# Attention weights rounded and split by two transfers instead of by engine instructions

## The chip, the cores and the metric

The kernel runs on one core of a Trainium2 chip. The metric is the device time of one execution in microseconds (us). The median of the runs decides. Next to it stands one profiled execution, whose trace gives the start and the duration of every instruction.

The engines of a core each work through their own instructions in order: PE (matmul), PEld (PE's loading of weights, beside the matmuls), DVE (vector), ACT (scalar and activation functions), POOL (general purpose) and SP (issues transfers). They wait for each other by semaphores. POOL and ACT can issue transfers as well.

## The reference

Two layers over a sequence of 512 tokens with 1024 channels. Per layer:

```
h = RMSNorm(x)
q, k, v, gates of 16 heads = h @ w_in           # one combined projection
A (8 heads): compressed, selected and window attention, gated
B (4 heads): stick-breaking attention           C (4 heads): forgetting attention
x = x + concat(A, B, C) @ w_out
x = x + cross_attention(RMSNorm(x), RMSNorm(mem), w_mq, w_mk, w_mv, w_mo)
x = x + (silu(gate) * val) @ w_down,  gate, val = conv3(RMSNorm(x) @ w_up)
```

and a last RMSNorm. All is in fp32.

## The kernel before

PE multiplies in a rounded fp32 format (`fp32r`). To keep the precision, each operand is split into a rounded part and the rest that rounding leaves, and each product is three matmuls: weight-high by input-high, weight-high by input-low, weight-low by input-high. A "weight" below is a block of a weight matrix, 128 partitions by 384 to 1120 columns, and takes two buffers of the kind `w`: `h` (rounded) and `l` (rest). There are NW = 8 of them (line 26). `load_w` (line 494) makes a weight in pieces of at most 560 columns: SP fetches a piece into a `raw` buffer (`wr` in the trace; six of them), ACT or DVE copies it to `h` with rounding, DVE or POOL writes raw minus `h` to `l`. Weights of 1024 to 1120 columns come in two pieces, those of 384 and 512 columns in one.

Per layer the weights are: 16 tiles of `w_in` (`job_t`) and three wider blocks, two weights each (`job_n`); the output projection in three parts, `wa` with eight weights of 512 columns and `wb` with eight of 384 (`job_wo`, line 1448), and one more of 1024; eight of the cross-attention, of 1024; then the feed-forward weights through `Prefetch` (line 519), two ahead.

Nothing is issued as written. Every operation is first recorded in a list (`Plan.add`, with a cost for its engine). `Plan.run` (line 207) then sets the order: for each engine it takes the ready operation of the lowest number in the list, and if none of the low ones is ready, a later one. An operation that needs a new buffer gets it if one of its kind is free and `room` finds that the operations ahead of it in the list can still go on with what remains. At the end it creates the buffers and issues the operations in that order (line 349). A buffer's name is its own number, an underscore, and a number that counts the buffers in the order of their creation. So `w1056_927` was created 927th, although the list names it late.

`run_items` mixes the projections (as filler) with the attention items, so that PE has matmuls of a projection while DVE and ACT work on a softmax.

Of the kernel before, what the change touches and what calls it, by code (L numbers as in the profile page):

```python
# [12 lines left out]
FR = mybir.dt.float32r  # L13
BF = mybir.dt.bfloat16
AF = mybir.ActivationFunctionType
OP = mybir.AluOpType
# [6 lines left out]
NF = 22  # L23
NH = 11

NSLOT, NW, NRAW = 67, 8, 6
WRAW = 560
EPS = 1e-6
NEG = -1e30
# [4 lines left out]
FPART, FNUM = 4, 2  # L34
# [318 lines left out]
class Engine:  # L353
# [17 lines left out]
    def __getattr__(self, name):  # L371
        def call(out, *args, **kw):
            full = lambda v: v.full if isinstance(v, Buf) else v
            out = full(out)
            args = [full(a) for a in args]
            kw = {k: full(v) for k, v in kw.items()}
            outs, ins = [out], [a for a in args if isinstance(a, View)]
            for k, v in kw.items():
                if isinstance(v, View):
                    (outs if k == "accum_out" else ins).append(v)  # L380
            real = lambda v: v.ap() if isinstance(v, View) else v
            eng = self.plan.engines[self.key]

            def fn():
                return getattr(eng, name)(real(out), *[real(a) for a in args], **{k: real(v) for k, v in kw.items()})  # L385

            if name == "activation" and args[1] in TABLED:
                ins = ins + [self.plan.table.full]
            if name == "dma_start":
                src = args[0]  # L390
                outs = [v for v in outs if isinstance(v, View)]
                size = ins[0] if ins else out
                nbytes = size.size() * (size.p1 - size.p0) * 4
                near = outs and ins and not any(v.buf.dram for v in outs + ins)
                cost = 1000 if self.key == "POOL" else 650 if near else 475
                if self.only:
                    return name, outs, ins, fn, cost, nbytes / 355.0
                return self.plan.add(self.key, name, outs, ins, fn, cost, nbytes / 355.0)
            if name == "matmul":
                n = args[1].size()  # L400
                c = max(64, n) / 2.4
                if args[1].buf.dtype == FT or (args[1].buf.dtype == FR and n < 256):
                    c *= 4
                if not kw.get("start"):
                    ins = ins + [out]
                return self.plan.add("PE", name, outs, ins, fn, max(c, 104) + 3)
            if name == "transpose":
                return self.plan.add("PE", name, outs, ins, fn, 110)
            cost = self._cost(name, out, ins, kw)
            if self.only:  # L410
                return name, outs, ins, fn, cost, 0
            return self.plan.add(self.key, name, outs, ins, fn, cost)
        return call
# [38 lines left out]
def tile_hybrid_trunk(ctx: ExitStack, tc: tile.TileContext, xT, memT, win_t, win_n0, win_n1, win_n2,  # L452
# [6 lines left out]
    plan = Plan(tc, {"slot": (NSLOT, sb), "w": (NW, sb), "raw": (NRAW, sb), "kcx": (1, sb),  # L459
                           "s32": (24, sb), "s128": (8, sb), "ps": (8, ps)})  # L460
    ve, se, te, gp, sy = [Engine(plan, k) for k in ("DVE", "ACT", "PE", "POOL", "SP")]
# [3 lines left out]
    def nm(s):  # L465
        uid[0] += 1
        return f"{s}{uid[0]}"
# [19 lines left out]
    def f(ap):  # L487
        return ap.bitcast(FT)
# [2 lines left out]
        te.matmul(o, a, b, start=start, stop=stop, skip_group_check=on)  # L491


    def load_w(src, n, shape, parts=None):

        h, l = [plan.buf("w", (128, n), FR, nm("w")).full for _ in range(2)]
        a, b = shape
        c = parts or -(-n // WRAW)
        if a == 1:
            cuts = [(src[:, :, k * b // c:(k + 1) * b // c], k * b // c, (k + 1) * b // c) for k in range(c)]  # L500
        else:
            cuts = [(src[:, k * a // c:(k + 1) * a // c], k * a // c * b, (k + 1) * a // c * b) for k in range(c)]

        def piece(v, c0, c1):
            def fn():
                raw = plan.buf("raw", (128, c1 - c0), FT, nm("wr"))
                sy.dma_start(raw, v)
                split(h[:, c0:c1], l[:, c0:c1], raw)
            return fn

        w = h.rearrange("p (a b) -> p a b", a=a), l.rearrange("p (a b) -> p a b", a=a)
        todo = [piece(*k) for k in cuts]
        if parts:
            return w, todo
        for t in todo:
            t()
        return w

    class Prefetch:
# [3 lines left out]

        def get(self, i):
            while self.n < min(len(self.specs), i + 1 + self.ahead):
                self.got[self.n] = load_w(*self.specs[self.n])
                self.n += 1
            return self.got.pop(i)

# [1065 lines left out]
    nrm = Norm(gn[:, 0, 0])  # L1595
    first, pieces = {}, []
    for tl in FIRST:
        first[0, tl], p = load_w(win_t[0, tl], 1024, (8, 128), FPART)
        pieces += p
    sy.dma_start(gn, gains)  # L1600
    for j in range(8):
# [105 lines left out]
```

## Time and profile before

| | us |
|---|---|
| median of three runs | 1523.96 |
| lowest run | 1519.58 |
| profiled execution, device time | 1528.35 |
| its span, first to last instruction | 1526.6 |
| PE busy | 1434.0 |
| DVE busy | 1142.1 |
| ACT busy | 678.0 |
| POOL busy | 428.7 |

The span runs through: start (0 to 58 us), attention of layer 1 mixed with its projections (to 309), the rest of the output projection (to 323), cross-attention (to 402), feed-forward (to 768), then the same for layer 2 (780 to 1512), and the output. An engine that is busy for less than the whole span is not the bound in general, but can be in a stretch. A matmul's row shows 0.39 us, but the next one starts 0.23 us after it, since matmuls are pipelined.

### The profile page before, as it was taken

How to read it: one execution, taken by the hardware profiler on the slowest of the kernel's cores; microseconds unless marked ns; L12 is line 12 of the kernel's file. 1: busy time of each engine (PE TensorE's matmuls, PEld its weight loads, DVE VectorE, ACT ScalarE, POOL GpSimd, SP SyncE). 2: the span in 40 equal slices, each digit the busy share in tenths (PEclk: the TensorE clock that was granted, in tenths of full speed). 3: DMA queues.
4: the chain of work that ended last, by engine and by line, in shares of the span. 5: the costliest groups of instructions: out<-in, count | busy, mean ns of one | idle time of the engine just before them, and what ended most of it. 6: DMA issues, size and time to landing. Idle time of an engine off the chain costs nothing.

```text
span 1526.6 us, 21518 instructions
## 1 busy us (share of the span) xinstructions
PE 1434.0 (94%) x7414; PEld 1171.9 (77%) x7414; DVE 1142.1 (75%) x2198; ACT 678.0 (44%) x1498; POOL 428.7 (28%) x357
## 2 busy tenths in 40 slices
PE   7789899888899999999999989999889999999997
PEld 5768687677788788888888767876878887888886
DVE  7997856888988835887577777576988786378864
ACT  5547566646632212323333656774584322132321
POOL 4440312342422212221143312133533221122211
PEclk9899999999999999999999999999999999999999
DMA  8630223134122233332443112312312223323232
GB/s 254 201 100 29 70 77 101 31 104 132 56 97 95 69 103 107 97 100 79 147 125 103 34 45 79 114 49 72 113 44 85 90 84 93 108 89 95 80 95 75
DMA packets 88205, 142.05 MB, mean 93 GB/s; under 512 B 12208, under 2 KB 35040, under 8 KB 88096
## 3 DMA queue, kind: packets, MB, share of 16 engines
q1 hardware_dynamic: 85280, 137.67, 29.1%
q0 software_dynamic: 1184, 1.44, 0.4%
q10 hardware_dynamic: 1632, 1.57, 0.3%
q8 instruction: 58, 0.95, 0.3%
q14 instruction: 51, 0.42, 0.1%
HBM read 125.04 MB, written 8.39 MB: 87 GB/s over the span
## 4 chain that ended last, share of the span: by engine, by line
PE 67%; DVE 23%; issue 4%; ACT 3%; DMA 1%; SPq 0%; POOL 0%; DVEq 0%; ACTq 0%; POOLq 0%
PE pj L385 37%; PE S L385 23%; PE acc L385 4%; DVE w L385 4%; DVE cv L385 3%; PE T L385 3%; DVE hl L385 2%; ACT cv L385 1%; DVE x L385 1%; DVE u L385 1%; DVE P L385 1%; DVE sp L385 1%; DMA wr<-in_dram 1%; DVE cs L385 1%; DVE sa L385 1%
## 5 line engine op out<-in xcount | busy, mean ns | idle before, releaser
L385 POOL TENSOR_TENSOR w<-wr,w 128x512 fp32r<-128x512 f32 (+4 forms) x217 | 304.6, 1409 | 825.4 <-PE pj L385 339.3
L385 PE MATMUL pj<-hh,w 128*128 128x512 f32 (+1 forms) x1376 | 433.0, 385 | 13.1 <-ACT hh L385 7.7
L385 PEld LDWEIGHTS pj<-hh,w 128*128 128x128 f32 x1376 | 255.5, 191 | 65.2 <-ACT hh L385 8.6
L385 ACT ACTIVATE w<-wr 128x512 fp32r<-128x512 f32 (+3 forms) x296 | 165.4, 585 | 277.4 <-PE pj L385 176.8
L385 PE MATMUL pj<-hl,w 128*128 128x512 f32 (+1 forms) x688 | 263.2, 383 | 3.1 <-DVE hl L385 2.9
L385 DVE TENSOR_TENSOR w<-wr,w 128x512 fp32r<-128x512 f32 (+3 forms) x251 | 195.0, 791 | 94.4 <-PE S L385 44.9
L385 PE MATMUL S<-hh,w 128*128 128x512 f32 (+1 forms) x736 | 230.7, 385 | 0.0
L385 DVE SCALAR_TENSOR_TENSOR cv<-u,conv,cv 128x510 f32<-128x510 f32 (+1 forms) x176 | 155.7, 887 | 69.8 <-ACT cv L385 66.6
L385 PEld LDWEIGHTS S<-hh,w 128*128 128x128 f32 x736 | 137.2, 189 | 29.6
L385 PEld LDWEIGHTS pj<-hl,w 128*128 128x128 f32 x688 | 131.3, 191 | 30.8 <-DVE hl L385 6.5
L385 DVE CAST w<-wr 128x512 fp32r<-128x512 f32 (+3 forms) x172 | 75.3, 453 | 97.0 <-issue 43.3
L385 ACT ACTIVATE cv<-u,conv 128x512 f32<-128x512 f32 x88 | 71.5, 815 | 171.1 <-DVE u L385 171.1
L385 PE MATMUL S<-hl,w 128*128 128x512 f32 (+1 forms) x368 | 141.4, 384 | 0.0
L385 PE MATMUL pj<-oh,w 128*128 128x512 f32 (+1 forms) x320 | 103.3, 374 | 18.1 <-DVE x L385 13.5
L385 PE MATMUL S<-gh,w 128*128 128x512 f32 (+1 forms) x396 | 114.3, 368 | 0.0
L385 PE MATMUL pj<-gh,w 128*128 128x512 f32 x352 | 113.4, 395 | 0.3 <-DVE gh L385 0.3
L385 ACT ACTIVATE P<-P,nmx 128x128 f32<-128x128 f32 (+3 forms) x160 | 88.5, 555 | 39.6 <-DVE nmx L385 39.3
L385 DVE CUSTOM_DVE_ANT_0 P<-S,maskq 128x128 f32<-128x128 f32 (+3 forms) x160 | 71.8, 483 | 40.1 <-PE S L385 37.8
L385 PEld LDWEIGHTS pj<-oh,w 128*128 128x128 f32 x320 | 60.3, 191 | 32.9 <-DVE x L385 15.8
L385 PEld LDWEIGHTS S<-gh,w 128*128 128x128 f32 x396 | 71.4, 188 | 13.4
L385 PEld LDWEIGHTS S<-hl,w 128*128 128x128 f32 x368 | 69.5, 189 | 15.0
L385 PE MATMUL pj<-w,hh 128*128 128x280 f32 (+2 forms) x384 | 79.4, 301 | 0.2 <-POOL w L385 0.2
(273 smaller groups left out, 2558.5 us busy)
## 6 DMA issues: line engine op xcount, KB each, us to landing
wr<-in_dram SPq DMA_DIRECT2D x292, 256.0 KB
wr<-in_dram SPq DMA_DIRECT2D x112, 192.0 KB
wr<-in_dram SPq DMA_DIRECT2D x48, 128.0 KB
x<-in_dram SPq DMA_DIRECT2D x16, 256.0 KB
dh<-dh SPq DMA_DIRECT2D x20, 128.0 KB
wr<-in_dram SPq DMA_DIRECT2D x8, 280.0 KB
wr<-in_dram SPq DMA_DIRECT2D x8, 260.0 KB
cw<-in_dram SPq DMA_DIRECT2D x8, 256.0 KB
```

The lines of the kernel that those rows point to most:

```text
L385: return getattr(eng, name)(real(out), *[real(a) for a in args], **{k: real(v) for k, v in kw.items()})
```

## The change

`load_w` is given a new body. POOL issues a transfer that brings the whole weight from memory into `h` and rounds it on the way; ACT copies `h` with the sign changed into `l`, in two halves; POOL issues a second transfer of the same weight, which adds it onto `l`. So `l` is again the weight minus its rounded part. No `raw` buffer, cast or subtract is used. The old body is kept as `split_w`, for the feed-forward weights (through `Prefetch`) and for the four tiles that are fetched at the very start. There are ten `w` buffers instead of eight and 62 buffers of the common kind (`slot`) instead of 67; the planner's cost for an issue by POOL goes from 1000 to 560 ns.

```
-NSLOT, NW, NRAW = 67, 8, 6
+NSLOT, NW, NRAW = 62, 10, 6
...
-                cost = 1000 if self.key == "POOL" else 650 if near else 475
+                cost = 560 if self.key == "POOL" else 650 if near else 475
...
-    def load_w(src, n, shape, parts=None):
+    def load_w(src, n, shape):
+        h, l = [plan.buf("w", (128, n), FR, nm("w")).full for _ in range(2)]
+        w = [v.rearrange("p (a b) -> p a b", a=shape[0]) for v in (h, l)]
+        gp.dma_start(w[0], src)
+        for c in range(2):
+            s_ = slice(c * n // 2, (c + 1) * n // 2)
+            se.activation(l[:, s_], f(h[:, s_]), AF.Copy, scale=-1.0)
+        gp.dma_start(w[1], src, accum_op=OP.add)
+        return w
+
+    def split_w(src, n, shape, parts=None):
...
-                self.got[self.n] = load_w(*self.specs[self.n])
+                self.got[self.n] = split_w(*self.specs[self.n])
...
-        first[0, tl], p = load_w(win_t[0, tl], 1024, (8, 128), FPART)
+        first[0, tl], p = split_w(win_t[0, tl], 1024, (8, 128), FPART)
```

The planner makes a new order out of it. Three places:

POOL in layer 1 at the end of the output projection, before (`w838`, `w842`, `w849`: the `l` buffers of `wb` weights):

```order
L385 TENSOR_TENSOR sp789_3289<-sp787_3241,sp788_3281 128x384
L385 TENSOR_TENSOR w838_3302<-wr839_2969,w837_3002 128x384
L385 TENSOR_TENSOR sb805_3335<-sp802_3271 128x256
L385 TENSOR_TENSOR sp811_3349<-sp809_3304,sp810_3342 128x384
L385 TENSOR_TENSOR sp809_3304<-sp809_3304,sb805_3335 128x256
L385 TENSOR_TENSOR w842_3373<-wr843_3015,w841_3225 128x384
L385 TENSOR_TENSOR w849_3487<-wr850_3090,w848_3368 128x384
```

and POOL at the same place now (`w802`, `w805`, `w808`, `w811` are `h` buffers of `wb` weights, `w797`, `w803`, `w806` `l` buffers, which the transfer adds onto):

```order
L385 DMA w802_3396<-in_7_dram 128x384
L385 DMA w794_3393<-in_7_dram 128x384
L385 DMA w805_3422<-in_7_dram 128x384
L385 DMA w797_3420<-in_7_dram 128x384
L385 DMA w808_3439<-in_7_dram 128x384
L385 DMA w803_3437<-in_7_dram 128x384
L385 DMA w811_3456<-in_7_dram 128x384
L385 DMA w806_3454<-in_7_dram 128x384
```

Subtracts among other work have become pairs of issues, the rounding transfer of one weight before the adding one of the weight ahead of it. By the creation numbers `w803` and `w808` come together, after `w797` and `w805`.

PE at that place before (`wb` weights `w837`/`w838` and `w841`/`w842`):

```order
L385 MATMUL pj840_3440<-oh819_3346,w837_3002 128x512
L385 MATMUL pj840_3440<-ol820_3377,w837_3002 128x512
L385 MATMUL pj840_3440<-oh819_3346,w838_3302 128x512
L385 MATMUL pj844_3455<-oh697_2929,w841_3225 128x512
L385 MATMUL pj844_3455<-ol698_2934,w841_3225 128x512
L385 MATMUL pj844_3455<-oh697_2929,w842_3373 128x512
```

and PE there now (`w796`/`w797` is one weight, `w802`/`w803` the next, `w808` the `h` of the weight next but one):

```order
L385 MATMUL pj798_3379<-oh722_3093,w797_3420 128x512
L385 MATMUL pj798_3379<-oh777_3305,w796_3351 128x512
L385 MATMUL pj798_3379<-ol778_3319,w796_3351 128x512
L385 MATMUL pj798_3379<-oh777_3305,w797_3420 128x512
L385 MATMUL pj810_3444<-oh661_2873,w808_3439 128x512
L385 MATMUL pj810_3444<-ol662_2881,w808_3439 128x512
L385 MATMUL pj804_3408<-oh661_2873,w803_3437 128x512
L385 MATMUL pj804_3408<-oh722_3093,w802_3396 128x512
```

`w803` gets its buffer when `w796` is read for the last time. Between that matmul and the first that reads `w803` stand three.

POOL early in layer 1, now, among the projections (`w186`, `w207` are `l` buffers of attention weights; `w1056` belongs to the first feed-forward weight):

```order
L385 DMA dl168_900<-dl168_900 64x512
L385 DMA dl170_907<-dl170_907 64x512
L385 TENSOR_TENSOR w1056_927<-wr1058_394,w1055_780 128x512
L385 DMA w186_923<-in_2_dram 128x1024
L385 DMA rot15_77<-u180_939 8x512 x2
```

and the first subtract of a feed-forward weight on POOL before, which stands behind the subtracts of the cross-attention's weights:

```order
L385 TENSOR_TENSOR w990_3986<-wr992_3637,w989_3890 128x512
L385 TENSOR_TENSOR w1069_4015<-wr1071_3895,w1068_3915 128x512
L385 TENSOR_TENSOR w1073_4020<-wr1074_3928,w1072_3980 128x512
L385 TENSOR_TENSOR sta955_3961<-qm953_3952,sta955_3961 64x256
L385 TENSOR_TENSOR w1126_4141<-wr1127_3999,w1125_4111 128x512
```

So the first feed-forward weight was created 4111th and 4141st, and is created 780th and 927th now.

## Rows read from the trace of the kernel before

**Rows 1.** The page, busy us, share of the span and instructions.

```profile
PE 1434.0 (94%) x7414; PEld 1171.9 (77%) x7414; DVE 1142.1 (75%) x2198; ACT 678.0 (44%) x1498; POOL 428.7 (28%) x357
```

**Rows 2.** Busy time by stretch: start:end, length, engines, granted clock, DMA share, GB/s.

```profile
core 0: us, PE busy (x) PEld busy (x) DVE busy (x) ACT busy (x) POOL busy (x), PEclk, DMA share, GB/s
58.00:116.00 58.00, 51.28 (x272) 41.86 (x272) 52.04 (x121) 29.06 (x76) 24.41 (x23) 0.94 0.51 156
116.00:309.00 193.00, 182.14 (x1086) 142.76 (x1085) 137.92 (x364) 127.72 (x320) 44.09 (x35) 1.00 0.21 62
309.00:323.00 14.00, 14.00 (x61) 11.16 (x62) 10.20 (x13) 3.62 (x6) 5.93 (x5) 1.00 0.43 138
323.00:402.00 79.00, 63.83 (x461) 58.92 (x460) 73.75 (x144) 51.88 (x138) 35.36 (x35) 0.92 0.32 102
402.00:768.00 366.00, 365.04 (x1639) 298.28 (x1638) 264.07 (x406) 112.60 (x185) 81.52 (x59) 1.00 0.32 98
780.00:1055.00 275.00, 257.81 (x1486) 206.20 (x1485) 199.37 (x494) 156.83 (x391) 77.36 (x64) 0.98 0.23 69
1069.00:1158.00 89.00, 74.24 (x539) 69.09 (x538) 83.81 (x170) 56.48 (x149) 39.10 (x38) 0.92 0.25 76
1158.00:1512.00 354.00, 353.60 (x1542) 286.48 (x1541) 247.44 (x376) 99.80 (x159) 76.85 (x54) 1.00 0.28 88
```

**Rows 3.** Waits of PE: for whom, us in total, times, longest.

```profile
PE pj L385 <- DVE x L385: 18.4, 12, 3.1
PE T L385 <- DVE P L385: 9.4, 10, 1.4
...
PE pj L385 <- DVE w L385: 1.1, 2, 0.6
...
PE pj L385 <- POOL w L385: 0.2, 1, 0.2
```

**Rows 4.** Groups of instructions: count, busy us, mean ns; idle before.

```profile
L385 POOL TENSOR_TENSOR w<-wr,w 128x512 fp32r<-128x512 f32 (+4 forms) x217 | 304.6, 1409 | 825.4 <-PE pj L385 339.3
L385 DVE TENSOR_TENSOR w<-wr,w 128x512 fp32r<-128x512 f32 (+3 forms) x251 | 195.0, 791 | 94.4 <-PE S L385 44.9
L385 DVE CAST w<-wr 128x512 fp32r<-128x512 f32 (+3 forms) x172 | 75.3, 453 | 97.0 <-issue 43.3
...
L385 ACT ACTIVATE w<-wr 128x512 fp32r<-128x512 f32 x190 | 114.0, 625 | 148.2 <-PE pj L385 102.7 <-issue 24.5 <-PE S L385 7.8
...
L385 ACT ACTIVATE w<-wr 128x256 fp32r<-128x256 f32 x21 | 8.7, 413 | 22.2 <-PE pj L385 17.5 <-issue 3.5 <-DMA wr<-in_dram 1.2
```

**Rows 5.** Tiles `rot`, then `dl`: POOL's issues, ns min/median/max, and landing.

```profile
L385 POOL DMA_DIRECT2D rot<-u x22: 497/514/546, 33.0 to 847.1; - x22
...
DMA to landing us min/median/max: 1.8/2.4/5.3
...
L385 POOL DMA_DIRECT2D dl<-dl x4: 527/537/558, 98.8 to 990.4; - x4
...
DMA to landing us min/median/max: 2.3/3.8/4.0
```

**Rows 6.** The page, transfer queue of SP: packets, MB, share of 16 engines.

```profile
q1 hardware_dynamic: 85280, 137.67, 29.1%
```

**Rows 7.** Timeline at the end of `wb`: start, duration, instruction [idle before].

```profile
320.44 0.39 PE L385 MATMUL pj<-ol,w 128*128 128x512 f32 x1
...
320.67 0.63 PE L385 MATMUL pj<-oh,w 128*128 128x512 f32 x2
...
320.92 0.64 ACT L385 ACTIVATE w<-wr 128x512 fp32r<-128x512 f32 x1 [1.43 <-PE pj L385]
...
321.63 1.29 POOL L385 TENSOR_TENSOR w<-wr,w 128x512 fp32r<-128x512 f32 x1 [0.75 <-ACT w L385]
...
321.94 1.25 DVE L385 CAST w<-wr 128x512 fp32r<-128x512 f32 x1
```

**Rows 8.** The chain that ended last, matmuls of 256 columns: start, us, count.

```profile
349.40 5.49 PE pj L385 x48
```

## What the change is expected to do to the time

> **What bounds the kernel now.** I read the page's busy shares first: PE is busy 1434.0 of 1526.6 us, DVE 75%, ACT 44%, POOL 28% [rows 1]. Then the table by stretches [rows 2]: in the feed-forward stretches (402 to 768 and 1158 to 1512) PE is free for about 1 us. In the attention stretches (116 to 309, and 780 to 1055 in layer 2) it is free for 11 us of 193 and 17 of 275. The 14 us from 309 to 323, which are the second part of the output projection (`wb`, eight weights), have no gap at all. Only in the cross-attention stretches (323 to 402, 1069 to 1158) is DVE the fuller engine, 73.75 of 79.00 us, with PE free for 15. Last the waits [rows 3]: PE waits for `x` and `P`; for a weight it waits 1.1 us (DVE) and 0.2 us (POOL) in the whole run. So the weights come in time today, and the work that makes them lies beside PE's wherever DVE is not the bound.
>
> **What is removed.** Of 468 pieces, 148 go (attention weights; SP's `wr` transfers fall from 468 to 320). By the order on each engine DVE loses 74 casts and 76 subtracts, ACT 74 copies, POOL 72 subtracts. By mean durations that is DVE 74 x 0.453 + 76 x 0.791 = 94 us and POOL 72 x 1.409 = 101 us [rows 4]. Where it could pay is PE's free time in the stretches with such weights: 6.7 + 10.9 + 15.2 us in layer 1 and 17.2 + 14.8 in layer 2, together 64.8 [rows 2]. Bounds of the gain: 0 (PE hardly waits for weights) and 65. I take 50, near the upper end, because whatever of this free time a lighter DVE leaves over can serve the new waits below; it can't be lost twice.
>
> **What is added.** 90 weights, each with two transfers issued by POOL and two ACT copies. POOL's issue: the rows of `rot` and `dl` show about 0.5 us each [rows 5], 180 x 0.54 = 97 us, as much as it loses, and beside PE. ACT: 116 halves of 512 columns (some a little wider) at 0.625, 32 of 256 at 0.413, 32 of 192 at some 0.36 (estimate, on the line through the other two) [rows 4], 97 us more, less the 74 copies that go: ACT, busy for 128 of 193 us at most [rows 2], has room. The weights' bytes are read twice: about 38 MB more beside 142, where the DMA engines are busy for 0.21 to 0.51 of the time [rows 2]. None of this is the price. The price is time from slot to weight, and how many weights are under way.
>
> **How many are under way.** A weight needs two of the `w` slots, 8 before and 10 now. But the attention weights no longer pass through the six `raw` buffers, so SP fetches feed-forward pieces as soon as layer 1 begins, and engines with nothing of lower number to do split them. The POOL rows in the section on the change show `w1056`, a feed-forward weight, made as tile 927, while PE reads it after the whole cross-attention. Six slots go so in layer 1 (`w1055`, `w1056`, `w1059`, `w1060`, `w1063`, `w1064`, all made by tile 1667) and six in layer 2 (`w2542` to `w2554`). Four slots stay: two weights under way, where before it was four. The negated copy of the next weight can't be written before PE has finished with the one ahead of it: it takes that one's slot.
>
> **Time from slot to weight.** Before: the raw piece lies ready, ACT copies in 0.625 us and POOL subtracts in 1.409, or DVE does both in 0.453 + 0.791 [rows 4]: 1.2 to 2.1 us. Now: handovers, two ACT halves, issue and landing of the adding transfer. The handovers I take as 0.35 us: 0.16 because a matmul ends 0.39 us after its start while the next follows after 0.23, and 0.07 for each step, as from ACT's end at 321.56 to POOL's start at 321.63 [rows 7]. The landing no row shows. Nearest are POOL's own transfers: 16 KB land 1.8 to 5.3 us after issue, median 2.4; 128 KB 2.3 to 4.0, median 3.8 [rows 5]. For the bytes: q1 moved 137.67 MB in 29.1% of 16 engines' time, 3.23 us a MB [rows 6]. An addition reads its target too: between the same rate and half of it. Bounds: 1.8 us + 3.23 a MB, and 3.8 us + 6.46 a MB. I take 2.4 us + 4.85 a MB, the median of the most numerous rows and the middle rate: 3.4 us for 197 KB, 3.7 for 262 KB, 4.9 for 524 KB. For weights of 384, 512 and 1024 columns the whole comes to 0.35 + 0.72 + 3.4 = 4.4, 0.35 + 0.83 + 3.7 = 4.9 and 0.35 + 1.25 + 4.9 = 6.5 us.
>
> **What lies over it.** In PE's order I counted the matmuls between the one that frees the slot and the first that reads the adding transfer's result, at 0.23 us for 512 columns [rows 7] and 0.114 for 256 (48 in 5.49) [rows 8]. In `wb` there are three, 0.7 us (the PE rows in the section on the change; 0.88 on the mean over eight). In the first part of the output projection, `wa`, 3.35 on the mean. For projections mostly 2.4 to 5.8. In the cross-attention 0.1 to 7, mean 3.9. Weight by weight, a wait already made counting as cover for later ones, the waits are then: `wb` 8 x (4.4 - 0.88) = 28 us in each layer; `wa` 8 x (4.9 - 3.35) = 12 in each; projections 17 x 1.8 = 31 in layer 1 and 22 x 2.6 = 57 in layer 2 (which starts with its slots already gone); cross-attention (with the last block of the output projection) 9 x 3.1 = 28 in each. Sum 225 us. With the lower landing 138, with the upper 387.
>
> **Who is behind it.** POOL and ACT run in order: behind a copy that waits for PE stand `Exp` and the evictions, behind an adding transfer `rot`, `dh` and the squares' sums. PE is waiting for that weight anyway, so I add nothing.
>
> **The clock.** From 323 to 402 PE was busy for 63.83 of 79.00 us and the granted clock was 0.92, that is, partly at 1.2 and mostly at 2.4 GHz; in the dense stretches 1.00 [rows 2]. The attention stretches become like that: 440 us of PE work at about 5% more is 20 us; bounds 0 and 35 (8%).
>
> **Sum.** The profiled execution took 1528 us, its span being 1526.6; the median of the runs is 1524, 4 lower. 1528 - 50 + 225 + 20 = 1723, against the median 1719. Lower end: 138 - 65 + 0 = +73, 1597. Upper: 387 - 50 + 35, about 1896.
>
> **A rule beside it.** The Trainium skill (DMA: Bandwidth & Descriptors, section on the anatomy of a DMA on the SWDGE path) gives a GpSimd-issued transfer some 2.0 us and its bytes at 436 GB/s. By it the waits would sum to 127 us and the time to about 1620. The trace speaks for more: 16 KB would land in 2.04 us and took 2.4, 128 KB in 2.3 and took 3.8 [rows 5].
>
> **Rivals.**
> *Faster.* The transfers land so early that the order's cover is enough, and DVE's 94 us count. The waits fall under 50 us only if landing takes less than about 1.0 us plus 1 us a MB (counted as above: 53); from there the gain of up to 65 decides: about 1480 to 1490. Against it: no transfer of POOL's landed under 1.8 us.
> *No difference.* Landing near 1.2 us plus 1.5 a MB gives 69 us of waits, which the 65 of free time take up: 1524 to 1550. Against it the same rows, and `wb`, where there is no free time and 14 to 16 us would be lost in each layer.
> *Much slower.* POOL's issue or landing grows when DVE is busy, to the upper landing: waits of 300 to 390 us, 1850 to 1900. For it: a DVE cast beside a POOL subtract took 1.25 us where 0.453 is the mean [rows 4, 7], so the two do stand in each other's way. Against it: POOL's 22 `rot` issues lie between 497 and 546 ns with DVE busy three quarters of the time [rows 5]. The Trainium skill (SBUF — State Buffer, section on the two sides) says that GpSimd cannot write descriptors while VectorE runs a copy in its two-port mode; by it this rival's landing holds wherever a cast runs. The even issue rows agree with it only in part.
>
> **Chances.** Forecast, two weights under way and waits of 110 to 350 us: 0.74, within 1590 to 1850. The same mechanism, smaller, 1555 to 1590: 0.06. Much slower, beyond 1850: 0.05. No difference: 0.08. Faster: 0.07. The range 1555 to 1850 leaves out 2 in 10. A measurement here can tell about 2%: faster 0.07, within 2% 0.08, slower 0.85.
>
> **What would show it.** PE's waits name `DMA w<-in_dram`, 200 us or more in all, none in feed-forward, whose stretches keep 366 and 354 us. `wb` takes about 14 + 28 = 42 us in both layers, with eight gaps of 3 to 4 us. POOL's `w<-in_dram` issues take 0.5 to 0.7 us, landing 3 to 6. The clock falls under 1.00 in attention. Wrong would be: landing under 2 us; `wb` still dense; feed-forward stretches that change; issues of several us.

## The result, and the profile of the changed kernel

The changed kernel takes 1888.13 us (median of four runs, 1883.65 to 1891.67) against 1524.88 us of the kernel before: 1.239 times as long, with an interval of 1.237 to 1.242. (One of the four runs of the kernel before took 4902.57 us; the ratio leaves it out.) That it would be slower was forecast; 1719 us was not enough, and 1888 lies outside the range of 1555 to 1850. The profiled execution took 1883.65 us, its span 1881.5.

The engines first, the row of the page that answers to [rows 1]:

```profile
PE 1554.8 (83%) x7414; PEld 1241.8 (66%) x7414; DVE 1026.1 (55%) x2064; ACT 714.8 (38%) x1597; POOL 452.4 (24%) x483
```

PE does the same 7414 matmuls and is busy for 120.8 us longer. DVE has 116 us less to do. The rest of the longer span is idle time of PE: 326.7 us, where it was 92.6.

Then by stretch. The limits are landmarks of the program, so that the same work stands in each row to within 16 matmuls: attention with its projections, the two larger parts of the output projection (`wa` and `wb`), the rest of it with the cross-attention, and feed-forward, for layer 1 and then layer 2. First the kernel before, cut in this way:

```profile
58.00:254.50 196.50, 183.98 (x1085) 147.37 (x1086) 150.95 (x423) 121.08 (x321) 51.00 (x43) 0.98 0.33 97
254.50:323.10 68.60, 63.54 (x333) 48.51 (x332) 49.32 (x74) 39.42 (x80) 23.43 (x21) 1.00 0.19 59
323.10:402.10 79.00, 63.83 (x462) 58.92 (x461) 73.75 (x145) 51.78 (x138) 35.36 (x35) 0.92 0.32 102
402.10:768.80 366.70, 365.74 (x1645) 298.98 (x1645) 264.11 (x405) 113.14 (x185) 82.32 (x59) 1.00 0.31 98
768.80:997.70 228.90, 216.75 (x1263) 175.73 (x1261) 166.81 (x441) 123.47 (x323) 62.37 (x51) 0.98 0.27 81
997.70:1069.30 71.60, 66.56 (x340) 51.15 (x339) 50.08 (x79) 40.68 (x82) 24.46 (x21) 0.98 0.20 61
1069.30:1146.80 77.50, 63.94 (x460) 59.40 (x459) 72.45 (x144) 51.71 (x138) 35.90 (x35) 0.91 0.25 78
1146.80:1515.80 369.00, 367.40 (x1650) 299.65 (x1650) 259.91 (x405) 105.69 (x173) 81.36 (x59) 1.00 0.28 86
```

The same eight stretches of the changed kernel (columns as in [rows 2]; the number ahead of the DMA share is the granted clock):

```profile
58.00:312.00 254.00, 204.56 (x1085) 159.54 (x1085) 138.49 (x421) 122.97 (x321) 48.73 (x61) 0.90 0.42 103
312.00:449.00 137.00, 90.03 (x347) 61.34 (x345) 35.84 (x61) 44.67 (x103) 27.94 (x37) 0.78 0.32 61
449.00:559.70 110.70, 68.20 (x446) 63.68 (x447) 58.37 (x131) 52.11 (x138) 32.70 (x42) 0.76 0.45 100
559.70:929.50 369.80, 368.10 (x1646) 300.30 (x1646) 265.00 (x403) 113.01 (x186) 89.29 (x67) 1.00 0.33 100
929.50:1250.00 320.50, 251.94 (x1263) 196.78 (x1261) 141.89 (x428) 130.91 (x336) 55.76 (x78) 0.86 0.41 93
1250.00:1384.00 134.00, 89.06 (x352) 60.24 (x350) 36.27 (x62) 45.60 (x105) 28.24 (x38) 0.80 0.33 63
1384.00:1496.20 112.20, 69.86 (x447) 65.15 (x448) 59.89 (x132) 51.63 (x137) 35.09 (x42) 0.76 0.40 87
1496.20:1867.40 371.20, 368.33 (x1650) 299.49 (x1649) 243.62 (x348) 123.40 (x212) 102.48 (x79) 1.00 0.27 85
```

Feed-forward, whose weights were left as they were, keeps its time to 3 us. All else grows: 57.5, 68.4 and 31.7 us in layer 1, 91.6, 62.4 and 34.7 in layer 2. `wa` and `wb` take about twice their time. And the clock, which was 0.98 to 1.00 outside the cross-attention (0.91 and 0.92 there), is now 0.76 to 0.90 wherever attention weights are used: PE works there partly at 1.2 GHz.

Whom PE waits for, the view of [rows 3]:

```profile
PE pj L385 <- DMA w<-in_dram: 239.5, 92, 8.8
PE pj L385 <- DVE x L385: 8.6, 5, 2.6
```

The wait for weights, 1.3 us before, is now 239.5 us in 92 pieces, the longest 8.8 us. The wait for `x`, the largest one before, fell from 18.4 to 8.6. That fits DVE's relief, and it is small beside the new wait.

What the issues and landings cost: POOL's view of the tile `w` (ns: least, median, most), and the sizes with the median from issue to landing:

```profile
L385 POOL DMA_DIRECT2D w<-in_dram x180: 530/871/1292, 3.2 to 1479.2; - x180
...
DMA to landing us min/median/max: 2.5/4.6/11.2
```

```profile
w<-in_dram POOLq DMA_DIRECT2D x100, 512.0 KB, 5.7
...
w<-in_dram POOLq DMA_DIRECT2D x32, 256.0 KB, 4.0
...
w<-in_dram POOLq DMA_DIRECT2D x32, 192.0 KB, 3.3
```

These medians hold rounding and adding transfers together. By the order of the program, in which each weight's rounding transfer comes before its adding one, they can be told apart: the rounding ones landed after 2.6, 3.0 and 4.4 us (192, 256 and 512 KB, medians of 16, 16 and 50), the adding ones after 3.9, 4.4 and 6.7.

Last, one weight of `wb` in the timeline (start, duration, instruction, idle time before it):

```profile
421.46 0.63 PE L385 MATMUL pj<-oh,w 128*128 128x512 f32 x1
421.75 0.62 ACT L385 ACTIVATE w<-w 128x192 fp32r<-128x192 f32 x2 [7.65 <-issue]
...
422.39 1.45 POOL L385 DMA_DIRECT2D w<-in_dram  x2 [6.82 <-PE pj L385]
...
425.22 0.77 PE L385 MATMUL pj<-oh,w 128*128 128x512 f32 x1 [3.13 <-DMA w<-in_dram]
...
427.00 1.19 PE L385 MATMUL pj<-oh,w 128*128 128x512 f32 x2 [0.59 <-DMA w<-in_dram]
...
429.69 0.63 PE L385 MATMUL pj<-oh,w 128*128 128x512 f32 x1
429.98 0.62 ACT L385 ACTIVATE w<-w 128x192 fp32r<-128x192 f32 x2 [7.62 <-issue]
```

This is the chain that the prediction described, link by link. The last matmul on one weight starts at 421.46; ACT writes the negated copy into the buffer that it frees; POOL issues two transfers in 1.45 us, the rounding one for a later weight first and the adding one behind it. PE waits 3.13 us for the first, does two matmuls, waits 0.59 us for the second, and does the rest; then the next copy begins. From copy to copy it is 8.23 us, for nine matmuls that took 2.1 us before [rows 7]. What the prediction did not see is in the durations: after the waits the matmuls come every 0.43 us, not 0.23. Of 8.23 us, 3.7 are waits, and nine matmuls at the slow rate are 3.9. The adding transfer of this weight alone:

```profile
L385 POOL DMA_DIRECT2D w<-in_dram x1: 920/920/920, 422.9 to 422.9; - x1
...
DMA to landing us min/median/max: 3.9/3.9/3.9
```

### The profile page after: what moved, and what is told of

It reads as the page before. It is cut to its first block, busy times and chain, and to the rows that moved or that the text cites. A ratio compares the mean times of both kernels' runs of the same rounds, so it can differ in the third digit from the quotient of the medians.

```text
span 1881.5 us, 21535 instructions
## 1 busy us (share of the span) xinstructions
PE 1554.8 (83%) x7414; PEld 1241.8 (66%) x7414; DVE 1026.1 (55%) x2064; ACT 714.8 (38%) x1597; POOL 452.4 (24%) x483
## 5 line engine op out<-in xcount | busy, mean ns | idle before, releaser
L385 PE MATMUL pj<-hh,w 128*128 128x512 f32 (+1 forms) x1376 | 460.8, 411 | 97.9 <-DMA w<-in_dram 88.6
L385 POOL TENSOR_TENSOR w<-wr,w 128x512 fp32r<-128x512 f32 (+2 forms) x145 | 196.0, 1356 | 560.0 <-PE pj L385 218.8
L385 POOL DMA_DIRECT2D w<-in_dram x180 | 131.8, 743 | 618.4 <-PE pj L385 379.5
L385 ACT ACTIVATE w<-w 128x512 fp32r<-128x512 f32 (+4 forms) x180 | 89.1, 539 | 368.6 <-PE pj L385 225.7
L385 PE MATMUL pj<-oh,w 128*128 128x512 f32 (+1 forms) x320 | 132.2, 468 | 111.5 <-DMA w<-in_dram 100.1
L385 ACT ACTIVATE w<-wr 128x512 fp32r<-128x512 f32 (+2 forms) x222 | 118.5, 564 | 197.2 <-PE pj L385 100.9
L385 DVE TENSOR_TENSOR w<-wr,w 128x512 fp32r<-128x512 f32 (+2 forms) x175 | 125.3, 724 | 86.2 <-PE S L385 38.4
L385 DVE TENSOR_TENSOR x<-x,pj 128x512 f32<-128x512 f32 (+1 forms) x80 | 46.0, 575 | 196.3 <-PE pj L385 196.2
L385 ACT ACTIVATE P<-P,nmx 128x384 f32<-128x384 f32 (+3 forms) x160 | 88.2, 552 | 26.3 <-DVE nmx L385 25.7
L385 DVE CUSTOM_DVE_ANT_0 P<-S,maskq 128x384 f32<-128x384 f32 (+3 forms) x160 | 71.3, 485 | 45.9 <-PE S L385 44.2
```

## The experiments

**Which part of the path, and how many buffers.** The waits have two roots: few buffers, since feed-forward weights hold six of ten, and a long path from a free buffer to a finished `l`. In between lies a third thing, which the order of POOL shows: the planner gives a free buffer to whatever can use it at once, and that is the `h` of a later weight; the `l` of the next one, which needs its `h` landed, comes last. The first three runs take these apart.

The first lets feed-forward weights be made only after the copies of the layer's last attention weight:

```
-            se.activation(l[:, s_], f(h[:, s_]), AF.Copy, scale=-1.0)
+            gate[0] = se.activation(l[:, s_], f(h[:, s_]), AF.Copy, scale=-1.0)
...
-                split(h[:, c0:c1], l[:, c0:c1], raw)
+                cp = an.copy(h[:, c0:c1], raw, ("ACT", "DVE"))
+                if gate[0] is not None:
+                    plan.after(cp, gate[0])
+                an.tt(l[:, c0:c1], raw, f(h[:, c0:c1]), OP.subtract, ("DVE", "POOL"))
```

> The changed kernel, but the rounded copy of a feed-forward weight may be planned only after the negated copies of the last attention weight of its layer, so that feed-forward weights take no `w` buffers early. Theory (few slots): ten buffers instead of four serve the attention weights, but `h` buffers are still filled far ahead and take nine of them, so the `l` of the next weight still comes at the last moment in `wb` (three matmuls, 0.7 us, between its buffer's release and its first read, as before) and in much of the cross-attention, while in layer 2's projections the cover grows from 4.4 to 17 us. Counted in the same way as in the prediction (0.35 us, copies, 2.4 us + 4.85 a MB), the waits sum to 132 us instead of 225; with the clock's loss in proportion the run takes 1700 to 1760 us. `wb` stays at about 8 us a weight, the projections of layer 2 lose nearly all of their 56 us. Rival (the transfers are too slow however many buffers there are): within 2% of 1888 us, layer 2's projections as slow as in the changed kernel.

1751.07 us, 1.149 times the kernel before (1.144 to 1.154), inside the theory's range. Its waits for weights:

```profile
PE pj L385 <- DMA w<-in_dram: 145.2, 45, 8.4
```

132 were expected. A `wb` weight of layer 1 takes 9.2 us (seven copies from 359.65 to 414.61 us), where about 8 were expected. Taking away the early feed-forward weights alone gives back 137 us of the 363; more than half of the loss stays.

The second makes `h` and `l` halves of one buffer, so that a weight has room for both from the start, and leaves the feed-forward weights early:

```
-        h, l = [plan.buf("w", (128, n), FR, nm("w")).full for _ in range(2)]
+        w2 = plan.buf("w", (128, 2 * n), FR, nm("w"))
+        h, l = w2[:, :n], w2[:, n:]
```

(the same line in `split_w`, and `NW // 2` buffers of the kind).

> The changed kernel, but `h` and `l` of a weight are the two halves of one buffer (five double ones instead of ten), so a weight has room for both from the start; feed-forward weights are still taken early (three double buffers), two are left. Theory (few slots, and a path from free buffer to weight that is longer than PE's work on one weight): now the whole chain, rounding transfer, copies, adding transfer, begins only when the weight two ahead is done: about 3.3 + 0.7 + 3.3 = 7.3 us in `wb` against 2.1 us of PE's work on one weight, 4.0 + 0.8 + 4.0 in `wa`, 5.7 + 1.2 + 5.7 for 1024 columns against 5.5. So it is no better than the changed kernel and rather worse: 1880 to 2100 us, `wb` 9 to 10 us a weight. Rival (what hurts is only that `l` gets its buffer last): clearly faster than 1888, 1600 or less.

1759.56 us, one run. Neither held. The timeline shows what I had left out: the two double buffers become free close together, so the paths of two weights run side by side, and a `wb` weight takes 5.6 us on the mean instead of 8.23 (the copies of three successive pairs begin at 339.5, 350.7 and 361.9 us). The waits:

```profile
PE pj L385 <- DMA w<-in_dram: 157.9, 75, 5.7
```

The third has both edits.

> Both edits together: feed-forward weights not before the last attention weight's copies, and double buffers for `h` with `l`, five of them. Theory (few slots): four weights are made while PE works on one; in `wb` 4 x 2.1 = 8.3 us of cover against a path of 7.3 to 8, for 1024 columns 22 us against 13. The waits for `DMA w<-in_dram` fall from 240 us to under 40, the granted clock in the attention and output-projection stretches goes back to 0.97 or more, and the time to 1490 to 1570 us, that is, within some per cent of the kernel before, with a chance to be under it since DVE has 94 us less to do. Rival (the transfers themselves are the price: POOL's issues of 1.4 us a pair, landings of 3 to 7 us, DMA traffic): 1700 us or more, waits on weights of 120 us or more.

1537.57 us, 1.008 times the kernel before (1.005 to 1.012): inside the theory's range, far from the rival's. With room for five weights, each with its `l`, the same transfers, copies and additions cost next to nothing in waits, and the clock comes back (0.974 over the span, 0.898 in the changed kernel):

```profile
PE pj L385 <- DMA w<-in_dram: 16.1, 6, 4.4
```

With enough buffers, given in pairs, the transfers, copies and additions cost 13 us; the other 350 us appear only with the buffers as the changed kernel has them. The next run shows that they are not the price of the buffers alone either.

**The path alone.** In the changed kernel the second transfer only brings the weight, without adding, and the copies go:

```
-        for c in range(2):
-            s_ = slice(c * n // 2, (c + 1) * n // 2)
-            se.activation(l[:, s_], f(h[:, s_]), AF.Copy, scale=-1.0)
-        gp.dma_start(w[1], src, accum_op=OP.add)
+        gp.dma_start(w[1], src)
```

> The changed kernel, but the second transfer only brings the weight into `l`, rounded, without adding, and without the two negated copies ahead of it: `l` no longer depends on `h` (the output is therefore not the reference's). Buffers as in the changed kernel: feed-forward weights taken early, four left. Theory (the price of a weight is the length of the path from free buffer to `l` over PE's cover): the path loses the copies (0.7 to 1.25 us), the adding issue's longer time (0.9 against 0.54 us) and the addition; the waits, counted as in the prediction with 1.8 to 2.4 us + 3.23 a MB, are 107 to 146 us instead of 240, and the slower clock falls in proportion (about half a us for each us of waiting): 1680 to 1750 us. Rival (the copies and the addition cost little, the landing of any transfer is the matter): 1820 us or more.

1511.14 us, 0.993 times the kernel before (0.991 to 0.996). Both expectations were far off.

```profile
PE pj L385 <- DMA w<-in_dram: 33.1, 33, 3.3
```

Six buffers are still held by feed-forward weights (by 124 us eight casts and four subtracts of 512 columns are done for them: four `h` and two `l`), four are left, and yet 33 us of waits remain of 240. I had shortened the path and kept the order. But the order changes too: `l` waits for nothing but its buffer now, so POOL's order has `h` and `l` of one weight next to each other, and both are under way while PE works on the weight ahead. I take it that the dependence of `l` on `h` put `l` last and made its path run while PE waits; the run takes out the dependence, the copies and the addition at once, so it does not tell them apart. With e2_pair beside it: of the changed kernel's 240 us, giving `l` its buffer together with `h` takes away 82, and the rest of the step to e5_plain another 125. In another sequence the shares would come out otherwise: the causes act together and do not add.

**Buffers alone.** In the kernel before, four of the eight buffers are held by empty ones from the projections until the last product of the cross-attention:

```
+        held = [plan.buf("w", (128, 8), FT, nm("w")) for _ in range(4)]
+        for d in held:
+            gp.memset(d, 0.0)
         run_items(items, fill, lead=1, spread=SPREAD)
...
+        g0 = len(plan.ops)
         add_product(wm, 4, om, nrm3, HALVES)
...
+        for d in held:
+            plan.after(gp.memset(d, 0.0), plan.ops[g0])
```

> The kernel before (weights split by engines, no transfers by POOL for them), but four of its eight `w` buffers are held by empty buffers from the first projections of each layer until the last product of its cross-attention, as the feed-forward weights hold six of ten in the changed kernel. Theory (few slots alone do little; it is few slots and a long path together): the path from free buffer to `l` is 0.35 us + 0.5 to 0.6 (copy) + 0.7 to 1.4 (subtract), 1.6 to 2.4 us, against 0.9 us of cover in `wb` and 3 to 6 elsewhere: waits on weights of 20 to 80 us and half as much by the clock, 1545 to 1640 us. Rival (the number of slots is the whole price): 1750 us or more.

1547.01 us, 1.017 times the kernel before (1.014 to 1.019), as the theory had it. The two largest of its waits for weights:

```profile
PE pj L385 <- POOL w L385: 10.9, 14, 1.3
...
PE pj L385 <- DVE w L385: 7.4, 7, 2.5
```

With a path estimated at 1.6 to 2.4 us four buffers are nearly enough. Few buffers alone cost 24 us, and together with the long path 363.

**What DVE's relief is worth.** Double buffers, late feed-forward weights, and a second transfer that adds nothing: no engine works on attention weights.

```
-        for c in range(2):
-            s_ = slice(c * n // 2, (c + 1) * n // 2)
-            gate[0] = se.activation(l[:, s_], f(h[:, s_]), AF.Copy, scale=-1.0)
-        gp.dma_start(w[1], src, accum_op=OP.add)
+        gate[0] = gp.dma_start(w[1], src)
```

> The kernel with double buffers and late feed-forward weights, but the second transfer brings the weight into `l` without adding and there are no copies, so that ACT and DVE have no work on attention weights at all and POOL only issues (the output is not the reference's). It is the most that relieving DVE could bring. Theory A (the prediction's term: 94 us less on DVE turn 50 of the 65 us of PE's free time in the attention and cross-attention stretches into gain): 1460 to 1490 us. Theory B (PE's free time there comes from chains of dependent steps, each waiting for the one before, which a less busy DVE doesn't shorten): 1505 to 1535 us, PE's free time outside the feed-forward stretches within 15 us of the kernel before.

1484.30 us, 0.975 times the kernel before (0.973 to 0.977). This is in the range of theory A: 38 us under the kernel before, where the prediction's term had 50. PE's idle time falls from 92.6 to 60.3 us, and PE is busy for 10.8 us less:

```profile
PE 1423.2 (96%) x7414; PEld 1164.6 (79%) x7414; DVE 1011.2 (68%) x2130; ACT 607.2 (41%) x1359; POOL 404.6 (27%) x470
```

But this is more than the relief of DVE, and it bounds the prediction's term from above: ACT makes no copies either (607.2 us; 714.8 in the changed kernel), and nothing is added. Where DVE is as light and the copies and additions are made, in e3_both, PE's idle time apart from the waits for weights is 76.5 us instead of 91.3, and the time no better than before:

```profile
PE 1443.3 (94%) x7414; PEld 1181.0 (77%) x7414; DVE 1013.5 (66%) x2138; ACT 681.5 (44%) x1532; POOL 437.8 (29%) x472
```

So a gain was there to be had where weights come in time and no engine works on them; with the copies and additions as the change has them, no run shows it.

**The clock.** Eight more matmuls on resident data ahead of each `wa` and `wb` weight:

```
                 o = psum("pj")
+                oh = OT[KORD[k0]][0]
+                for _ in range(8):
+                    mm(o, oh[:, 0:128], oh, start=True, stop=True)
```

> The changed kernel with eight more matmuls (128x512, of a resident attention output with itself, overwritten by the real product) ahead of each of the 32 `wa` and `wb` weights: 256 matmuls, 59 us of PE work at 0.23 us each. They fall where PE waits for weights. Theory (the clock of 1.2 GHz there comes from PE's gaps, and the slow clock is a cost of its own): the clock of the `wa`/`wb` stretches rises from 0.78 to 0.95 or more, the real matmuls come every 0.23 us instead of 0.42, and these stretches get shorter although they hold more work: 137 and 145 us become 110 to 125, the whole run 1830 to 1865 us. Rival (the clock is low there for another reason, or its loss is hidden under the waits): the clock stays, the added matmuls run at 0.42 us and the stretches stay as long or grow by up to 20 us each, 1885 to 1930 us.

1906.02 us (1.250, 1.242 to 1.258): the time is in the rival's range, the clock in neither's. Inconclusive. The clock of the two stretches rose, from 0.78 and 0.80 to 0.87 and 0.89, but they also got longer, from 137 and 134 to 148 and 142.5 us: ahead of the `wa` weights PE often does not wait (five times from 312 to 376 us in the changed kernel), and there the added matmuls can only stand in its way. So the next run adds them ahead of the 16 `wb` weights only (`range(8 if k0 == NA else 0)`).

> The changed kernel with eight more matmuls (128x512, on resident data, overwritten by the real product) ahead of each of the 16 `wb` weights only, where PE waits for every weight; 128 matmuls in all. Theory (the slow clock costs time of its own, because PE's matmuls on the last weight stand in the path of the next one's buffer): the clock in the `wb` stretches rises from 0.61 to 0.9 or more, a weight takes 6.7 us instead of 8.25, so 12 us less in each layer and 1855 to 1875 us in all, although the kernel does 128 matmuls more. Rival (the loss of clock lies hidden under the waits, or has another cause than PE's gaps): 1885 us or more.

1875.90 us (four runs, 1868.59 to 1881.11): 12.2 us less than the changed kernel, whose four runs lie between 1883.65 and 1891.67, with 128 matmuls more. Each against the kernel before, it is 1.232 (1.228 to 1.236) beside 1.239 (1.237 to 1.242): some 10 us by this measure, and the intervals just miss each other. Six weights of `wb` in layer 1 and seven in layer 2, from copy to copy; first the changed kernel, then this one:

```profile
382.20:429.98 47.78, 25.91 (x67) 15.36 (x66) 4.82 (x7) 4.29 (x13) 8.68 (x12) 0.61 0.28 50
1316.39:1374.36 57.97, 31.76 (x80) 19.82 (x80) 5.51 (x8) 4.91 (x15) 10.14 (x14) 0.63 0.29 54
```

```profile
384.90:426.82 41.92, 31.83 (x130) 22.20 (x128) 4.82 (x7) 4.31 (x14) 8.70 (x12) 0.96 0.33 57
1309.71:1361.06 51.35, 36.36 (x143) 25.91 (x142) 5.51 (x8) 4.92 (x16) 10.17 (x14) 0.87 0.32 60
```

The clock goes from 0.61 and 0.63 to 0.96 and 0.87. A weight takes 6.99 and 7.34 us instead of 7.96 and 8.28, and 6 x 0.97 + 7 x 0.94 = 12.4 us, for these 13 of 16 weights, is most of the 15.1 us by which the two profiled executions differ (1883.65 and 1868.59). In one such weight of this kernel the matmuls come every 0.23 us again:

```profile
403.71 0.70 PE L385 MATMUL pj<-oh,w 128*128 128x512 f32 x2 [1.30 <-DMA w<-in_dram]
...
404.47 0.63 PE L385 MATMUL pj<-oh,w 128*128 128x512 f32 x2
...
405.17 0.39 PE L385 MATMUL pj<-oh,w 128*128 128x512 f32 x1
```

So the slow clock came from PE's own gaps, and it cost time beside the waits: the matmuls that read a weight stand in the path of the next one's buffer, and at 1.2 GHz that part of the path is twice as long.

**The rounding transfer alone.** The kernel before with only the first half of the change: `h` by POOL's transfer, `l` as before from a raw piece. (The planner's cost for an issue by POOL is 560 ns, as in the change.)

```
+        gp.dma_start(w[0], src)
...
-                split(h[:, c0:c1], l[:, c0:c1], raw)
+                an.tt(l[:, c0:c1], raw, f(h[:, c0:c1]), OP.subtract, ("DVE", "POOL"))
```

> One half of the change alone, on the kernel before (eight buffers, 67 slots): the rounded part of each attention weight is made by POOL's rounding transfer, the rest as before, a raw piece fetched by SP and subtracted by DVE or POOL; no negated copy, no adding transfer. The raw pieces stay in use, so feed-forward weights are not taken early. Theory (the price of the change is the path `h` lands, two copies, adding transfer lands, on buffers that are given to it last; the rounding transfer alone, issued far ahead, is not): from free buffer to `l` it is one subtract again, 0.7 to 1.4 us; waits on weights under 30 us. What it can gain is DVE's 74 casts (33 us of the 94 that gave 39 us in the run with free weights), so 10 to 15 us: 1500 to 1530 us. Rival (any weight that comes through POOL's transfers comes late, as `h` now lands 3 to 7 us after its buffer is free instead of 0.6): waits of 60 us or more, 1560 us or more.

1542.12 us, 1.011 (1.009 to 1.013). On the waits the theory held: 2.6 us for weights in all, so the rounding transfer, issued far ahead, costs none. On the time neither did. DVE got hardly any relief, because the planner took most of the missing casts from ACT (296 casts there become 182) and gave DVE more subtracts (212.4 us instead of 195.0):

```profile
L385 DVE TENSOR_TENSOR w<-wr,w 128x512 fp32r<-128x512 f32 (+2 forms) x257 | 212.4, 842 | 120.0 <-PE pj L385 57.4 <-PE S L385 40.3 <-issue 10.5
...
L385 DVE CAST w<-wr 128x512 fp32r<-128x512 f32 (+2 forms) x138 | 57.7, 433 | 58.0 <-issue 31.7 <-PE pj L385 12.4 <-PE S L385 7.3
```

Why it is 17 us slower, and not level, isn't settled; of PE's waits the one for `cs` is longer in the new order (15.3 us, 7.1 before).

The same with `h` and `l` in one buffer, four double ones:

> The same half of the change with `h` and `l` as halves of one buffer, four double buffers. Theory: as long as three weights can be made ahead of the one in use the order of giving buffers matters little when the path is short: within 1% of the run with single buffers, 1495 to 1535 us. Rival (late `l` buffers were still costing something, or the longer hold of a double buffer costs): more than 1% apart.

1547.89 us, 1.015 (1.013 to 1.017): within 0.4% of the run before it, as the theory had it, though both lie above its range in us. With a short path the order in which buffers are given matters little.

**Towards a version that beats both.** 53 us lie between e3_both and e7_free. The first attempt takes POOL's small transfers from behind the adding ones (`on=("SP",)` in `Any.dma`), on the kernel of e3_both.

> The kernel with double buffers and late feed-forward weights, with all small transfers (`dh`, `dl`, `dhl`, `rot`) issued by SP and none by POOL, where an adding transfer that waits for its copies holds up what stands behind it. Theory (53 us lie between that kernel and the one whose weights need no copies and no addition; part of it is POOL's queue, part ACT's copies): PE's waits for `DMA dh` and `DMA dl`, 8.6 us, go, and some of what hangs on them: 1520 to 1533 us, level with the kernel before. Rival (POOL's queue costs nothing but these waits, and SP's issues cost as much): 1533 to 1545 us.

1521.98 us, 0.998 times the kernel before (0.997 to 1.000, ten runs): 16 us less than e3_both and level with the kernel before. But not in the way expected. Of the 8.6 us of waits for `dh` and `dl`, 5.3 are still there:

```profile
PE S L385 <- DMA dh<-dh: 4.1, 1, 4.1
...
PE S L385 <- DMA dl<-dl: 1.2, 1, 1.2
```

The waits for weights rose from 16.1 to 23.0 us, and PE's idle time in the profiled execution from 92.6 to 95.4; what fell is PE's busy time, from 1443.3 to 1430.2. The planner's order changed with the edit, so whether POOL's queue was a part of the 53 us is open. The second lets DVE make negated copies as well:

> The same, and the negated copies may be made by DVE as well as by ACT (72 of 180 by the order). Theory (ACT's 97 us of copies, behind which exponentials and evictions stand, are the larger part of the 53 us): 1500 to 1525 us, under the kernel before by up to 1.5%. Rival (the 53 us come from the length of the path and the adding transfers, not from ACT): within 0.5% of the run with the copies on ACT alone.

1534.50 us, 1.007 (1.005 to 1.009), 0.8% slower than with the copies on ACT alone. Neither expectation held: giving DVE copies (85 of 180 in the trace) does not help. What copies that cost nothing would give isn't shown by it. The remaining 38 us against e7_free weren't traced further: the copies, the longer path (PE still waits 23.0 us for weights in e11_sp) and the adding transfers are left as candidates. Nor was the smaller number of common buffers, 62 instead of 67, varied by itself. No version that computes the reference was clear of the kernel before.

The waits and PE's busy time of these runs side by side (from each one's waits and page; PE was busy for 1434.0 us before):

| run | buffers left for attention | `l` gets its buffer | copies and addition | waits for weights | PE busy | time |
|---|---|---|---|---|---|---|
| changed kernel | 4 | last | yes | 239.5 | 1554.8 | 1888 |
| e2_pair | 4 | with `h` | yes | 157.9 | 1520.0 | 1760 |
| e5_plain | 4 | with `h` | no | 33.1 | 1431.1 | 1511 |
| e1_gate | 10 | last | yes | 145.2 | 1506.7 | 1751 |
| e3_both | 10 | with `h` | yes | 16.1 | 1443.3 | 1538 |
| e7_free | 10 | with `h` | no | 3.7 | 1423.2 | 1484 |

## Why the prediction was right and wrong

The span grew by 354.9 us. By its parts: waits for weights 239.5 - 1.3 = 238.2; PE busy 120.8 longer; PE's other idle time 91.3 to 87.2, 4.1 less. The sum of the prediction was 225 + 20 - 50.

- **Time from slot to weight, and what lies over it: the wait was right, its size partly by luck.** 225 us were forecast and 238 measured. By place, forecast and measured: projections of layer 1 31 and 31.5 us, of layer 2 57 and 56.2; `wa` and `wb` 40 in each layer, 42.0 and 42.8 measured; the rest up to feed-forward 28 in each, 32.5 and 32.2. But the path was longer than forecast: the landing of the adding transfer was taken as 3.4, 3.7 and 4.9 us by size and measured as 3.9, 4.4 and 6.7 in the median, and from the start of the copies to that landing it took 5.1, 5.7 and 8.7 us, where 4.4, 4.9 and 6.5 were forecast from a little earlier, the end of the matmul. One reason in `wb` is the rounding issue, which stands ahead of the adding one on POOL. That the waits came out right even so means that PE's work over the path was longer than counted, too: in `wb` its matmuls came every 0.43 us and not 0.23; elsewhere this wasn't traced. So `wb` took not 42 us but 64 to 66 (eight weights of 7.96 and 8.28 us): the waits were as forecast, the work beside them was not. By the Trainium skill (DMA: Bandwidth & Descriptors, section on the anatomy of a DMA on the SWDGE path) the landings would have been 2.5, 2.6 and 3.2 us, an estimate from its 2.0 us and 436 GB/s; the trace does not agree, and without the addition (2.6, 3.6 and 5.1 us in e7_free) only for the smallest.
- **How many are under way: right, but not the whole.** The feed-forward weights took the buffers as described; without that, in e1_gate, 137 us come back. That `h` buffers filled far ahead push `l` to the end was in the rows of the order that I showed, and I didn't name it as a cause of its own.
- **The clock: wrong by a factor of six, and the largest miss.** 20 us were forecast with 35 as the bound, 120.8 measured. I took the granted clock of the cross-attention before, 0.92 with PE busy for four fifths of the time, as what all attention stretches would fall to, and left `wb` and the cross-attention itself out of the 440 us. But the forecast's own waits left PE busy for a third of `wb` (14 us of work beside 28 of waits), a case that no row of before showed. There it fell to 0.61, and over `wa` and `wb` to 0.78 and 0.80. (Of the 120.8 us some are the longer first matmul after a gap, at most 92 x 0.16 = 15.) The bound was the step that failed: it came from one stretch with short gaps (3.1 us at most) and was used for stretches with longer ones (waits of up to 5.3 us in the projections of layer 1 and 7.5 in layer 2). For what was left out is only a part of the miss: PE's busy time grew by 20.6 and 35.2 us in the projections, by 26.5 and 22.5 in `wa` and `wb`, and by 4.4 and 5.9 in the cross-attention, where the clock had been low before. Over the runs the loss goes with the waits: PE busy grew by 72.7, 86.0 and 120.8 us with waits of 145, 158 and 240, half a us for each; by place it is some 0.6 in the projections and in `wa` and `wb`, and 0.1 to 0.2 in the cross-attention. In e5_plain, 33 waits of 1.0 us on the mean cost none of it.
- **What is removed: a second miss.** 50 us were taken. In the changed kernel PE's idle time apart from the waits for weights fell by 4. e7_free gives 38 us, but with ACT and POOL relieved as well; e3_both, with the copies and additions, gives 15 in PE's idle time and nothing in the whole. That a stretch in which PE waits for a weight has no use for a DVE that is done earlier is the likely reason in the changed kernel; no run tests it by itself. I had even written that the free time can't be lost twice, and then added gain and waits as if they lay in different places. The upper end of the sum, too, took 50 of gain where its own bound was 0; with 0 it would be 1946, not 1896.
- **What is added: right where it was called free, with one size off.** POOL's issues took 131.8 us and not 97: a rounding one some 0.54 to 0.57 us, an adding one some 0.9 (medians by size). Feed-forward kept its time, 3 us longer in layer 1 and 2 in layer 2.
- **The rivals.** The time lies in the range of "much slower", but not by its mechanism. The waits were 240 us, not 300 to 390, and the adding landings were longer than forecast whether DVE was busy or not: for 512 KB 6.6 us in the median where DVE was busy for more than half of the landing, 6.5 where for less than a quarter. The 28 issues during which DVE ran a cast or copy took no longer than the others (rounding 0.54 to 0.70 us, adding 0.87 to 0.95). Faster and no difference failed where the prediction said, in `wb` first.

With 121 us for the clock and 4 for the gain, both read from the result, the same sum gives 1528 + 225 + 121 - 4 = 1870. This is bookkeeping and shows where the miss lay; it does not test the sum.

## What to carry to other kernels

Where a resource is handed out by a list scheduler, look at who gets a free buffer, not only at how many there are: a step that can start at once (a load far ahead) takes the buffer from the one that is needed next but has to wait for its own input. Give both parts of a product their room together, and keep work of later stages out until it is near. When a forecast has PE waiting in a dense stretch, price the clock with it, from a row where PE waits as much, and don't count a gain on another engine in the same stretch.

## What was not expected of the hardware

An adding transfer cost POOL more to issue than a rounding one of the same size: 0.89 to 0.92 us beside 0.54 to 0.57 (medians by size, 192 to 512 KB), and it landed 1.3 to 2.3 us later after its issue. And matmuls without use made a kernel faster: 128 of them, placed in PE's gaps, raised the granted clock in `wb` from 0.61 and 0.63 to 0.96 and 0.87 and took 10 to 12 us off the time.
